# Projections, scores and transposes as pairs of half-row products

## The chip, the core and the metric

The kernel runs on one core of a Trainium2 chip, as one launch. TensorE multiplies, and writes its sums to eight banks of the accumulation memory, of 512 fp32 columns by 128 rows each. VectorE (DVE), ScalarE (ACT) and GpSimd (POOL) do the elementwise work, and all transfers are issued by SyncE (SP). The metric is the time of one execution on the device, in microseconds (us). Of the kernel before there are three runs: 823.28 us in the median, from 822.88 to 824.9.

## What is computed

One layer of a hybrid encoder, for 1024 prompt rows and 32 sample rows of width 1024, all in fp32. Cut to what matters:

```
hn = rmsnorm(h, g_pre)
qA kA vA gA qB kB vB gB = split(hn @ w_in)      # 8 parts of 512 columns
# A: 8 heads of 64, each 64-row chunk sees itself and the 8 chunks before
sA = qA @ kA.T / 8 + bias[clip(k_pos - q_pos, -128, 128)]
oA = softmax(where(in_band, sA, -1e30)) @ vA
# B: 8 heads of 64, strictly causal
z  = qB @ kB.T / 8
w  = sigmoid(z) * product of sigmoid(-z) over the later causal keys
oB = w @ vB
y  = concat(oA * silu(gA), oB * silu(gB)) @ w_out
h  = h + rmsnorm(y, g_post)
h  = h + sigmoid(h @ w_ple_gate) * (p @ w_ple)
```

The k and v of both halves are outputs too. The sample rows also attend to 512 cached keys per head.

## The kernel before

**Precision.** An fp32 matrix enters TensorE as two fp32r parts, an upper part `h` (the value rounded) and a lower part `l` (what rounding left over). A product of two such matrices is the sum of three: upper by upper, upper by lower, lower by upper.

**Projections.** The normed input, transposed, lies in three chunks `hnh[c]`, `hnl[c]` of 352 columns (1056 rows of prompt and sample). A kind (`kA`, `qA`, `vA`, `gA` and so on) and a head pair `p` give 128 output columns. `col_steps` (line 616) makes one kind of one head pair: for each chunk 24 products (3 combinations by 8 blocks of 128 input features) are summed in one bank with the tag `mm`, then ACT copies it to a staging tile `st`. With 32 kind-and-pair combinations and 3 chunks there are 96 such units, 2304 products. For a gate kind, the unit ends in a sigmoid, a multiplication on DVE, one on POOL by the attention's output, and a store.

**Attention.** `prep_k`, `prep_q`, `prep_v` (lines 560 to 582) lay out one head. A head is 64 wide, so q's upper and lower part are stacked in 128 rows (`L`), and k's upper part stands in both halves of `kd`, k's lower part in both halves of `kl`: one product with `kd` and one with `kl` give all combinations. For each block of 128 queries, `scores` (703) multiplies against all its key blocks: up to 5 in A, up to 8 in B, in one piece of up to 512 columns or in two. In A, DVE adds the bias and takes the maximum, ACT exponentiates, POOL scales. In B, DVE adds the mask, ACT takes two sigmoids, DVE runs a scan (the product over later keys), POOL multiplies. `weights_t` (746) transposes the resulting weights on TensorE, block by block of 128x128 against the identity `ident`, and ACT and DVE split the result into `wTh` and `wTl`. `values` (773) sums the weights by v over key blocks in the bank `PV`.

**Transposes elsewhere.** `turn_x` (521) transposes the normed input, `token_major` (587) the k and v that are stored, `sample_attention` (815) the cached k and its weights.

**Banks.** `PS_BUFS` (406) gives two banks to `mm`, three to scores `S`, two to transposes `T`, one to `PV`.

**Order.** All operations are recorded by `Recorder` and then put in order by its `order` (307): a planner that simulates the engines with fixed prices (`cost`, 274) and takes the ready operation of each engine by key. On TensorE attention has the key 0 and projections the key 1, so projections fill what attention leaves. Every recorded operation is issued from line 385, so all rows of the profile carry that line and are told apart by tile names. `weave` (1117) interleaves the attention of head pair n with the projections of pair n+1; pairs 0 to 3 are A, 4 to 7 B. `share = {7: 8}` (1051) places all eight gate combinations in the last pair's stretch, since it has no next pair. The last two gates are recorded after all attention (`GATE_NEEDS`), because their last multiplication needs the attention's output.

**After attention** come the output product and the gated embedding product, blocked into seven smaller products each (`o0P` to `o3P`, `g0P` to `g3P`, tags `ple`, `o`, `g`). The change leaves them as they are, but for the names of two bank tags.

Of the kernel before, what the change touches and what calls it, by code (L numbers as in the profile page):

```python
# [20 lines left out]
KD = 8  # L21
# [13 lines left out]
PARTS = 4  # L35
BEHIND = 2
# [120 lines left out]
class Op:  # L157
    __slots__ = ("eng", "what", "args", "kw", "key", "busy", "late", "ready", "left", "after", "at", "size", "shared")
# [5 lines left out]
ISSUE = 450  # L164
DMA_NS, DMA_RATE, DMA_MARGIN = 1500, 320.0, 800
# [34 lines left out]
class Recorder:  # L200
# [35 lines left out]
    def node(self, eng, what, args, kw, after):  # L236
        o = Op()
        o.eng, o.what, o.args, o.kw, o.after = eng, what, args, kw, after
        o.key = (self.cls if eng == "PE" else self.low, len(self.ops))
        o.shared = False  # L240
        self.ops.append(o)
        return o

    def add(self, eng, what, args, kw):
        writes, reads = [], []
        method = what[1] if isinstance(what, tuple) else ""
        for i, a in enumerate(args):
            if isinstance(a, (View, Raw)):
                (writes if i == 0 or (method == "tensor_tensor_reduce" and i == 7) else reads).append(a)
# [17 lines left out]
        o.busy, o.late = self.cost(eng, method, args, kw, writes, reads)  # L267
        o.shared = eng == "POOL"
# [38 lines left out]
    def order(self):  # L307
# [16 lines left out]
        out, port, line = [], 0.0, 0.0  # L324
        while len(out) < len(self.ops):
# [15 lines left out]
            if o.shared and e == "DVE" and port > t + DVE_SET:  # L341
                held = [x for x in now[e] if not x[2].shared]
                if held:
# [4 lines left out]
                    o = pick[2]  # L348
            o.at = t
# [25 lines left out]
    def emit(self, tc):  # L375
        ops = self.order()
        with tc.manual_schedule():
# [13 lines left out]
def stream_step(  # L391
# [14 lines left out]
    PS_BUFS = {"mm": 2, "S": 3, "T": 2, "PV": 1}  # L406

    def psum(tag, name):
        return ps.tile([P, 512], F32, tag=tag, name=name, bufs=PS_BUFS[tag])
# [31 lines left out]
    )  # L441
    masks = const.tile([P, NS], F32, tag="masks", name="masks")
# [64 lines left out]
    TURN = {}  # L507
# [13 lines left out]
    def turn_x(t, sq, n):  # L521
        for kh in range(2):
            pt = psum(TURN.get((t, kh), "T"), f"ptx{t}_{kh}")
# [31 lines left out]
    KDh, KLD, Lq, V2 = {}, {}, {}, {}  # L555
# [31 lines left out]
    def token_major(ab, p, src, nm, b0, then):  # L587
# [3 lines left out]
        def turn(g0):  # L591
# [3 lines left out]
            pt = psum("T", f"pt{nm}{ab}{p}_{g0}")  # L595
            if g0 < 8:
                for b in range(4):
                    nc.tensor.transpose(pt[:, b * P:(b + 1) * P], src()[:, (g0 + b) * P:(g0 + b + 1) * P], ident)
                nc.scalar.copy(out[:, g0:g0 + 4, :], pt.rearrange("p (b c) -> p b c", b=4))
            else:  # L600
                nc.tensor.transpose(pt[0:NS, 0:P], src()[:, SEQ:T], ident)
                nc.scalar.copy(out[0:NS, 8, :], pt[0:NS, 0:P])
                then(out)

        return [(0.43 if g < 8 else 0.1, lambda g=g: turn(g)) for g in range(b0, 9, 4)]
# [9 lines left out]

    def col_steps(j):

# [3 lines left out]
        box = {}  # L621
        steps = []

        def mms(c, part):
            if part == 0:
                if c == 0:
                    ensure(j)
                    ensure(j + 1)
                    if k != "g":
                        box["st"] = at2.tile([P, T], F32, tag="stg", name=f"st{kind}{p}", bufs=3)  # L630
                box["acc"] = psum("mm", f"mm_{kind}{p}_{c}")[:, 0:CH]
            acc = box["acc"]
            cs = slice(c * CH, (c + 1) * CH)
            if k == "g" and part == 0:
                box["og"] = at2.tile([P, CH], F32, tag="bias", name=f"og{kind}{p}_{c}", bufs=2)
                dma(box["og"], o_dr[n][:, cs])
            W = loaded[j]
            for x in range(part * 24 // PARTS, (part + 1) * 24 // PARTS):
                q, k8 = x // KD, x % KD
                a = W[k8 // 4][1 if q == 1 else 0]  # L640
                b = (hnl if q == 2 else hnh)[c]
                nc.tensor.matmul(acc, a[:, k8 % 4, :], b[:, k8, :], start=(x == 0), stop=(x == 23))
            if part < PARTS - 1:
                return
            if k == "g":
                sg = at2.tile([P, 512], F32, tag="sg", name=f"sg{kind}{p}_{c}", bufs=3)[:, 0:CH]
                nc.scalar.activation(sg, acc, AF.Sigmoid)
                nc.vector.tensor_tensor(sg, acc, sg, ALU.mult)
                nc.gpsimd.tensor_tensor(sg, sg, box["og"], ALU.mult)
                dma(og_dr[n, :, cs], sg)  # L650
            elif k == "q":
                nc.scalar.activation(box["st"][:, cs], acc, AF.Copy, scale=SCALE)
            else:
# [1059 lines left out]
```

## Time and profile before

| | |
|---|---|
| median of three runs | 823.28 us |
| profiled execution | 822.59 us |
| its span (first to last instruction) | 820.8 us |
| TensorE products | 4926, busy 811.7 us |
| TensorE weight loads | 4926, busy 751.1 us |
| DVE, ACT, POOL busy | 601.8, 496.1, 508.3 us |
| granted TensorE clock | 1.0 |
| moved by transfers | 127.19 MB |

Every product on TensorE is a pair of instructions: a weight load (PEld), which puts one matrix of up to 128 rows by 128 columns into the array, and the product itself (PE), which streams the columns of the other through it. A load can run under the product before it. In a row of the timeline `128*128 128x352` means 128 active rows by 128 active columns, and 352 streamed columns; `32*128 32x32` has 32 active rows. The ends of products are modelled, and neighbours overlap in the record, so the distance from start to start is read, and not the length of a single one. In the view of groups the columns are busy time, mean length in ns, then the engine's idle time before.

By the names of the tiles: the projections of the first head pair run to 63.5 us, attention from there to 590.8 us with projections between, the gates until 624 us (from 496.6 us), and the output and gate products to the end.

### The profile page before, as it was taken

Reading aid. Unit: us, or ns where it says so; the run is one execution under the profiler, and the core shown is the slowest. Engines: PE = TensorE matmul, PEld = TensorE weight load, DVE = VectorE, ACT = ScalarE, POOL = GpSimd, SP = SyncE. Lnnn points to the kernel's source line nnn. Section 1 sums busy time; section 2 is a strip of 40 time slices with the busy share of each in tenths; the row PEclk is TensorE's granted clock in tenths of the full one; section 3 lists DMA queues with packets and bytes.
Section 4 is the critical chain, followed back from the end, with each engine's and each line's share of the span. In section 5 each row is a group of like instructions: output and inputs, shape, how many; then the busy total and the mean of one; then the engine's idle time right before and its main releaser. Section 6 shows DMA issues by size and latency. Waiting matters only on the chain.

```text
span 820.8 us, 14862 instructions
## 1 busy us (share of the span) xinstructions
PE 811.7 (99%) x4926; PEld 751.1 (92%) x4926; DVE 601.8 (73%) x1197; ACT 496.1 (60%) x1145; POOL 508.3 (62%) x559
## 2 busy tenths in 40 slices
PE   9999999999999999999999999999999999999997
PEld 7999999999999999999999999999998787888786
DVE  6718886776677688898988889985654676686755
ACT  6624745655636667756665775663437966886741
POOL 6526775585766486675657856676463437599513
PEclk9999999999999999999999999999999999999999
DMA  9327544574545563312333233253479847749733
GB/s 309 109 70 249 145 143 146 146 204 146 147 120 171 144 174 96 85 33 67 105 89 82 50 105 92 83 150 111 135 258 303 287 143 243 251 156 362 245 117 128
DMA packets 113279, 127.19 MB, mean 155 GB/s; under 512 B 10850, under 2 KB 80266, under 8 KB 113203
## 3 DMA queue, kind: packets, MB, share of 16 engines
q1 hardware_dynamic: 113202, 126.24, 50.5%
q8 instruction: 39, 0.64, 0.3%
q14 instruction: 38, 0.30, 0.1%
HBM read 81.21 MB, written 36.59 MB: 144 GB/s over the span
## 4 chain that ended last, share of the span: by engine, by line
PE 94%; DVE 2%; POOL 1%; ACT 1%; DMA 1%; issue 0%; SPq 0%; DVEq 0%
PE mm_kB L385 6%; PE mm_gA L385 6%; PE mm_qA L385 6%; PE mm_kA L385 6%; PE mm_gB L385 5%; PE mm_qB L385 5%; PE mm_vA L385 5%; PE mm_vB L385 5%; PE PVB L385 4%; PE SB L385 4%; PE ptwB L385 4%; PE SA L385 4%; PE PVA L385 4%; PE ptwA L385 3%; PE g1P L385 2%; PE o3P L385 2%
## 5 line engine op out<-in xcount | busy, mean ns | idle before, releaser
L385 POOL TENSOR_TENSOR beB<-beB,omB 128x128 f32<-128x128 f32 (+7 forms) x64 | 87.5, 1373 | 78.6 <-DVE omB L385 25.0
L385 DVE TENSOR_TENSOR_SCAN omB<-omB 128x128 f32<-128x128 f32 (+7 forms) x64 | 100.1, 1575 | 4.4 <-ACT omB L385 2.2
L385 POOL TENSOR_SCALAR beA<-beA,statA 128x640 f32<-128x640 f32 (+2 forms) x64 | 44.3, 696 | 48.6 <-DVE statA L385 47.0
L385 ACT CAST wThA<-ptwA 128x128 fp32r<-128x128 f32 (+3 forms) x96 | 40.1, 424 | 37.4 <-PE ptwA L385 36.5
L385 ACT CAST wThB<-ptwB 128x512 fp32r<-128x512 f32 (+3 forms) x96 | 44.9, 487 | 24.7 <-PE ptwB L385 23.2
L385 ACT ACTIVATE omB<-SB 128x384 f32<-128x384 f32 (+5 forms) x96 | 47.4, 507 | 18.9 <-DVE SB L385 8.1
L385 DVE TENSOR_TENSOR wTlB<-ptwB,wThB 128x512 fp32r<-128x512 f32 (+3 forms) x96 | 50.7, 547 | 9.0 <-ACT wThB L385 7.2
L385 DVE TENSOR_TENSOR wTlA<-ptwA,wThA 128x128 fp32r<-128x128 f32 (+3 forms) x96 | 45.6, 485 | 15.7 <-ACT wThA L385 15.0
L385 ACT ACTIVATE beA<-omA,statA 128x640 f32<-128x640 f32 (+2 forms) x64 | 44.7, 699 | 9.4 <-DVE statA L385 3.5
L385 ACT ACTIVATE beB<-SB 128x384 f32<-128x384 f32 (+5 forms) x96 | 46.6, 506 | 3.4 <-DVE Vl2sB L385 2.0
L385 PE MATMUL ptwB<-ident,beB 128*128 128x128 f32 x288 | 45.0, 273 | 0.1
L385 PE MATMUL ptwA<-ident,beA 128*128 128x128 f32 x240 | 41.5, 273 | 0.0
L385 PEld LDWEIGHTS ptwB<-ident,beB 128*128 128x128 f32 x288 | 35.1, 140 | 2.3 <-issue 0.4
L385 PE MATMUL SB<-kdB,LB 128*128 128x384 f32 (+5 forms) x96 | 34.1, 358 | 0.5 <-ACT beB L385 0.5
L385 DVE CUSTOM_DVE_ANT_0 omA<-SA,biasA 128x320 f32<-128x320 f32 (+2 forms) x64 | 30.8, 481 | 4.5 <-PE SA L385 3.8
L385 PE MATMUL SB<-klB,LB 128*128 128x384 f32 (+5 forms) x96 | 33.4, 349 | 0.0
L385 PEld LDWEIGHTS ptwA<-ident,beA 128*128 128x128 f32 x240 | 30.7, 140 | 1.4 <-issue 0.2
L385 POOL TENSOR_TENSOR oB<-oB,oB 128x256 f32<-128x256 f32 x32 | 25.4, 815 | 10.2 <-issue 5.6
L385 PE MATMUL SA<-kdA,LA 128*128 128x320 f32 (+2 forms) x96 | 31.2, 332 | 0.5 <-DVE LA L385 0.4
L385 POOL TENSOR_TENSOR gB<-gB,gB 128x256 f32<-128x256 f32 x32 | 27.5, 878 | 6.3 <-DMA gB<-in_w_ple_gate_dram 6.1
L385 PE MATMUL SA<-klA,LA 128*128 128x320 f32 (+2 forms) x96 | 30.4, 324 | 0.0
L385 POOL TENSOR_TENSOR h<-h,x 128x512 f32<-128x512 f32 (+1 forms) x18 | 23.4, 1320 | 0.8 <-DVE h L385 0.8
(706 smaller groups left out, 2698.1 us busy)
## 6 DMA issues: line engine op xcount, KB each, us to landing
x<-in_x_prompt_dram SPq DMA_DIRECT2D x8, 512.0 KB, 5.5
oB<-in_w_out_dram SPq DMA_DIRECT2D x16, 256.0 KB, 4.5
sum_dro<-oB SPq DMA_DIRECT2D x16, 256.0 KB, 2.2
gB<-in_w_ple_gate_dram SPq DMA_DIRECT2D x16, 256.0 KB, 4.3
sum_drg<-gB SPq DMA_DIRECT2D x16, 256.0 KB, 2.1
x<-in_x_prompt_dram SPq DMA_DIRECT2D x16, 256.0 KB, 3.8
h_dr<-h SPq DMA_DIRECT2D x8, 512.0 KB, 3.5
ht<-h_dr SPq DMA_DIRECT2D x8, 512.0 KB, 5.1
```

Source lines behind the costliest of these rows:

```text
L385: getattr(getattr(tc.nc, o.what[0]), o.what[1])(*args, **kw)
```

## The change

**Half rows.** TensorE's array can be used as two halves of 64 rows, and the change issues most products as pairs: one product on rows 0 to 63, one on rows 64 to 127, each with a bank of its own (`pair`). Three kinds of work become pairs.

- A projection unit's 24 products are cut into 48 half products. Low rows and high rows of one pair belong to different units (`triple`): three units are open at once, and the high rows run `BEHIND` = 12 slots behind. A unit has one bank. It is summed first by one half of the rows, 24 products, and then by the other, and between them stands a `relay`: a one-element memset on POOL that waits for the last product of the one, and for which the first product of the other waits. There are three `mm` banks.
- A block of scores is three pairs (upper-upper, upper-lower, lower-upper): the low rows hold q against the first 64 keys of each key block, the high rows against the other 64. `prep_k` reorders k for this with two transfers, `prep_q` copies q's parts into the other half of the rows with two. The scores lie in two banks side by side (`SS`), and with more than four key blocks they take both whole.
- A transpose of a 128x128 block is two of 64 rows (`turn`), whose results lie in two banks (`TT`), in halves of 256 columns used in turn.

ACT's and DVE's instructions on scores and transposes span both banks, and where a block of scores had two pieces there is one instruction now. A bias of the A heads is loaded in two parts, in 64-column runs.

**Order.** The planner adds `CHANGE` = 170 when TensorE goes between half rows and full rows; the products of one `values`, and of one block of scores, are kept together (`together`, `in_turn`). The planner's prices for pairs are 158 for a projection, 61 for a transpose, and at least 107 for scores.

**Gates.** One gate each goes to the stretches of pairs 4, 5 and 6, and five stay in the last. The k and v transposes of a kind come two steps into the next kind's projections.

The transposes of the first three input tiles, of the sample rows' input and of the last phase, all values and the output products stay in full rows. The diff, cut to its core:

```diff
-PARTS = 4
-BEHIND = 2
+STEPS = 12
+BEHIND = 12
...
+    def pair(self, first, second, busy):
+
+        both = [x for x in (first, second) if x]
+
+        def emit(*real):
+            for i, (method, _, _, _, more) in enumerate(both):
+                more = dict(more)
+                bank = more.pop("bank", None)
+                done = getattr(self.tc.nc.tensor, method)(*real[3 * i:3 * i + 3], **more)
+                if bank is not None:
+                    if bank.count == 24:
+                        self.wait(done, bank.relay, "the other half of the rows has written this bank")
+                    bank.count, bank.last = bank.count + 1, done
+
+        args = [v for x in both for v in x[1:4]]
+        self.add("PE", emit, args, {})
+        self.ops[-1].busy = busy
+        return self.ops[-1]
...
+    def relay(self, bank, buf):
+
+
+        def emit(real):
+            bank.relay = self.tc.nc.gpsimd.memset(real, 0.0)
+            self.wait(bank.relay, bank.last, "a bank is handed to the other half of the rows")
...
+            if e == "PE" and o.mode != mode:
+                t, mode = t + CHANGE, o.mode
...
-    PS_BUFS = {"mm": 2, "S": 3, "T": 2, "PV": 1}
+    PS_BUFS = {"mm": 3, "PV": 1}
+    TT, SS = (TwoBanks(rec, ps, x) for x in ("TT", "SS"))
+    LOW, HIGH = slice(0, HD), slice(HD, P)
+    second = []
...
+    def turn(out, src, x):
+
+        n = src.shape[1]
+        rec.pair(*(("transpose", out[0:n, a, x * HD:(x + 1) * HD], src[r], ident[r, r], {}) for a, r in enumerate((LOW, HIGH))), 61)
...
     def prep_k(nm, h, st):
-        r, o = halves(h)
-        kd = opnd[h].tile([P, SEQ], F32R, tag=f"kd{h}", name=f"kd{nm}{h}")
-        kl = opnd[h].tile([P, SEQ], F32R, tag=f"kl{h}", name=f"kl{nm}{h}")
-        nc.vector.tensor_copy(kd[r], st[r, 0:SEQ])
-        nc.gpsimd.tensor_tensor(kl[r], st[r, 0:SEQ], f(kd[r]), ALU.subtract)
-        dma(f(kd[o]), f(kd[r]))
-        dma(f(kl[o]), f(kl[r]))
-        KDh[h], KLD[h] = kd, kl
+
+        K = opnd[h].tile([P, 2, 512], F32R, tag=f"L{h}", name=f"K{nm}{h}")
+        raw = wpool.tile([P, 512], F32, tag="wr", name=f"rk{nm}{h}", bufs=4)
+        src = st[h * HD:(h + 1) * HD, 0:SEQ].rearrange("p (b a k) -> p b a k", b=8, a=2)
+        for a, r in enumerate((LOW, HIGH)):
+            dma(raw[r].rearrange("p (b k) -> p b k", b=8), src[:, :, a, :])
+        nc.vector.tensor_copy(K[:, 0], raw)
+        nc.gpsimd.tensor_tensor(K[:, 1], raw, f(K[:, 0]), ALU.subtract)
+        Kq[h] = K
 
     def prep_q(nm, h, st):
         r, o = halves(h)
-        L = opnd[h].tile([P, SEQ], F32R, tag=f"L{h}", name=f"L{nm}{h}")
-        nc.vector.tensor_copy(L[r], st[r, 0:SEQ])
-        nc.vector.tensor_tensor(L[o], st[r, 0:SEQ], f(L[r]), ALU.subtract)
-        Lq[h] = L
+        qh = opnd[h].tile([P, SEQ], F32R, tag=f"kd{h}", name=f"qh{nm}{h}")
+        ql = opnd[h].tile([P, SEQ], F32R, tag=f"kl{h}", name=f"ql{nm}{h}")
+        nc.vector.tensor_copy(qh[r], st[r, 0:SEQ])
+        nc.vector.tensor_tensor(ql[r], st[r, 0:SEQ], f(qh[r]), ALU.subtract)
+        dma(f(qh[o]), f(qh[r]))
+        dma(f(ql[o]), f(ql[r]))
+        Lq[h] = (qh, ql)
...
+    def products(items):
+
+        for low, high in items:
+            behind.append(high)
+            x = [low, behind.pop(0)]
+            turned = [y[0].relay for y in x if y and y[0].count == 24]
+            now = rec.pair(*(y and y[0].product(y[1], r) for y, r in zip(x, (LOW, HIGH))), 158)
+            now.after.update(turned)
+            for y in x:
+                if y and y[0].count == 24:
+                    y[0].relay = rec.relay(y[0].bank, said)
+                if y and y[0].count == 48:
+                    y[0].end()
+
+    def triple(units):
+
+        low = [(u, x) for u in units for x in range(24)]
+        high = [(u, x) for u in (units[2], units[0], units[1]) for x in range(24)]
+        todo = list(zip(low, high))
+        m = len(todo) // STEPS
+        return [todo[m * t:m * t + m] for t in range(STEPS)]
...
+    def in_turn(begin):
+
+        rec.together(begin)
+        mine = [o for o in rec.ops[begin:] if o.eng == "PE"]
+        mine[0].after.update(scored)
+        scored[:] = mine[-1:]
...
-                bias = at2.tile([P, 640], F32, tag="bias", name=f"bias{nm}", bufs=2)
-                dma(bias, bias_src(2 * p + h, P, 0, 640))
-                nc.gpsimd.memset(bias[0:HD, 0:HD], NEG)
-                nc.gpsimd.memset(bias[HD:P, 576:640], NEG)
+                bias = at2.tile([P, 2, 320], F32, tag="bias", name=f"bias{nm}", bufs=2)
+                src = bias_src(2 * p + h, P, 0, 640).ap
+                for a in range(2):
+                    part = bass.AP(tensor=src.tensor, offset=src.offset + a * HD, ap=[[1, P], [P, 5], [1, HD]])
+                    dma(bias[:, a, :].rearrange("p (x k) -> p x k", k=HD), Raw(r_dr, part))
+                nc.gpsimd.memset(bias[0:HD, 0, 0:HD], NEG)
+                nc.gpsimd.memset(bias[HD:P, 1, 256:320], NEG)
                 box["bias"] = bias
 
...
-            L, kd, kl = Lq[h], KDh[h], KLD[h]
+            q, K = Lq[h], Kq[h]
             b0 = lo_block(i)
-            n = (i + 1 - b0) * P
-            k0 = b0 * P
-            cut = [0, n] if n <= 512 else [0, n // 2, n]
+            m = i + 1 - b0
+            n = m * P
             w0 = at.tile([P, SEQ + 1], F32, tag="om", name=f"om{nm}_{i}", bufs=3)
             w1 = at.tile([P, SEQ], F32, tag="be", name=f"be{nm}_{i}", bufs=3)
-            pieces = []
-            for j in range(len(cut) - 1):
-                s = psum("S", f"S{nm}_{i}_{j}")[:, 0:cut[j + 1] - cut[j]]
-                lhs = L[:, i * P:(i + 1) * P]
-                ks = slice(k0 + cut[j], k0 + cut[j + 1])
-                nc.tensor.matmul(s, lhs, kd[:, ks], start=True, stop=False)
-                nc.tensor.matmul(s, lhs, kl[:, ks], start=False, stop=True)
-                pieces.append((cut[j], cut[j + 1], s))
+            s = (SS.half if m <= 4 else SS.both)(f"S{nm}_{i}")[:, :, 0:m * HD]
+            lhs, ks = slice(i * P, (i + 1) * P), slice(b0 * HD, (i + 1) * HD)
+            begin = len(rec.ops)
+            for x, (y, z) in enumerate(((0, 0), (0, 1), (1, 0))):
+                more = dict(start=x == 0, stop=x == 2)
+                rec.pair(*(("matmul", s[:, a, :], q[y][r, lhs], K[r, z, ks], more) for a, r in enumerate((LOW, HIGH))), max(107, 5 + 0.4167 * m * HD))
+            in_turn(begin)
...
                 nc.gpsimd.memset(w0[:, n:n + 1], 1.0)
-                for a, b, s in pieces:
-                    nc.scalar.activation(w0[:, a:b], s, AF.Sigmoid, scale=-1.0)
-                for a, b, s in pieces:
-                    nc.scalar.activation(w1[:, a:b], s, AF.Sigmoid)
+                nc.scalar.activation(rows(w0[:, 0:n]), sv, AF.Sigmoid, scale=-1.0)
...
-                pt = psum("T", f"ptw{nm}_{i}_{j}")
+                pt = TT.half(f"ptw{nm}_{i}_{j}")
                 for x in range(m):
-                    nc.tensor.transpose(pt[:, x * P:(x + 1) * P], w1[:, (b - b0 + x) * P:(b - b0 + x + 1) * P], ident)
-                hi, lo = wT[g, j]
...
-    share = {7: 8}
+    share = {4: 1, 5: 1, 6: 1, 7: 5}
```

More of the change, by code (lines that the diff above doesn't have):

```diff
@@ new lines, in triple, with flush @@
+    def triple(units):
[4 more added lines that the diff above has]
+        return [todo[m * t:m * t + m] for t in range(STEPS)]
+    def flush():
+        rest = [(None, None)] * BEHIND
+        return [(0.95, lambda: products(rest[0:6])), (0.95, lambda: products(rest[6:]))] + [x for t in tails[0:1] for x in t]
+    def col_steps(j):
+        kind, p = order[j]
+        need = GATE_NEEDS.get((kind, p))
+        steps = [(0.95, lambda x=x: products(x), need if i == 0 else None) for i, x in enumerate(triple([Unit(j, c) for c in range(NCH)]))]
+        if tails:
+            steps[2:2] = tails.pop(0)
+        if kind[0] != "g":
+            tails.append(tail(j))
+        return steps
@@ L620, in col_steps @@
         n = sidx(ab, p)
[L621 to L653, printed above, removed]
-                nc.scalar.copy(box["st"][:, cs], acc)
@@ L1234, in stream_step @@
     ensure(2)
-    first = [col_steps(j) for j in range(3)]
+    first = [triple([Unit(j, c) for j in range(3)]) for c in range(NCH)]
     for c in range(NCH):
@@ L1239, in stream_step @@
                 norm_tile(t, *(xs.get(t) or load_x(t)), GPRE)
-        for j in range(3):
-            for st in first[j][PARTS * c:PARTS * (c + 1)]:
-                st[1]()
+        for x in first[c]:
+            products(x)
     for x in ple.later:
```

262 lines of the change are left out of this document (195 added, 67 removed).

## The prediction

> **What bounds the kernel now.** I read the page's busy times and slices first, then the chain that ended last, then TensorE's list of waits, and last the pieces of the chain and the timeline, where the pace of one kind of product can be read.
>
> ```profile
> PE 811.7 (99%) x4926; PEld 751.1 (92%) x4926; DVE 601.8 (73%) x1197; ACT 496.1 (60%) x1145; POOL 508.3 (62%) x559
> PEclk9999999999999999999999999999999999999999
> PE 94%; DVE 2%; POOL 1%; ACT 1%; DMA 1%; issue 0%; SPq 0%; DVEq 0%
> PE idle L385 <- DVE newh L385: 1.3, 1, 1.3
> PE PVsB L385 <- DVE Vl2sB L385: 0.9, 2, 0.5
> ```
>
> TensorE is busy 811.7 of 820.8 us at the full granted clock, makes 94% of the chain, and the two largest sums in its list of waits are 1.3 and 0.9 us. So the span is TensorE's instructions laid end to end, and a change is priced by what it takes from or adds to that row of instructions. A mean duration of a product overlaps its neighbours; the pace is what counts, and merged runs give it:
>
> ```profile
> 32.33 3.90 PE mm_vA L385 x24
> 703.63 0.87 PE pth L385 x8
> 779.88 2.80 PE g3P L385 x12
> ```
>
> A 352-column projection product takes 3.90/24 = 0.1625 us, a 512-column one 2.80/12 = 0.233 us, a transpose of a 128x128 fp32 block 0.87/8 = 0.109 us. Between the first two a column costs 0.00044 us, so 320, 384 and 448 columns cost 0.148, 0.176 and 0.205 (worked out). Short products have a floor, the weight load:
>
> ```profile
> 302.33 0.19 PEld L385 LDWEIGHTS PVA<-wThA,v2A 128*128 128x128 f32 x1
> 302.44 0.30 PEld L385 LDWEIGHTS PVA<-wTlA,v2A 128*128 128x128 f32 x2
> 5.61 0.29 PEld L385 LDWEIGHTS gpre<-ghl,ones 1*128 1x128 f32 x2 [0.17 <-issue]
> 743.16 0.57 PEld L385 LDWEIGHTS pth<-ident,ht 32*128 32x128 f32 x8 [0.37 <-PE g1P L385]
> L385 PEld LDWEIGHTS ptwB<-ident,beB 128*128 128x128 f32 x288 | 35.1, 140 | 2.3 <-issue 0.4
> ```
>
> Two loads for fp32r products start 0.30 - 0.19 = 0.11 us apart with 128 rows, and 0.29 - 0.19 = 0.10 us apart with one row: the load's time does not shrink with the rows. Loads for transposes of 32 rows start (0.57 - 0.14)/7 = 0.061 us apart.
>
> **The change part by part.** In the order in which the changed program stands, TensorE has 8362 products instead of 4926: 4608 half-row projection products (2304 before), 816 half-row score products (384), 1456 half-row transposes in place of 728 full ones. Values, output and gate products stay full.
>
> *Projections.* 2304 full products become 2304 pairs of 352 columns, plus 12 slots because the second halves run 12 behind. If the two halves of a pair run side by side, a pair costs what one costs now, 0.1625. Bounds: below, 0.155 (a half streams the same 352 columns, so no gain beyond a few ns of issue); above, two loads one after the other, 2 x 0.11 = 0.22. I take 0.1625, because the 352 columns cover one load (0.11) with 0.05 to spare and the halves use different rows and banks: +12 x 0.1625 = +1.9 us. No row of this trace shows two halves at once; this is the large unknown.
>
> The TensorE page of the Trainium skill ("TensorE: Matmul & The Clock Gate", LDWEIGHTS) says that load time depends on the columns and not on the rows; the one-row load above agrees, and this speaks against the change, since a pair has two loads of full length. The skill's "TensorEngine Tiling (Array Packing)", Key Properties, says that different tiles load and multiply in parallel. By the second the term is +1.9, by the first with the loads in a row it is the rival below, +132.
>
> *Scores.* Before, q's upper and lower parts were stacked in 128 rows against k's upper part and then its lower part: 2 products over all n columns. Now three pairs (upper-upper, upper-lower, lower-upper) over n/2 columns in each half. Per A head before: 2 x (0.11 + 0.120 + 0.176 + 0.233) for the first four blocks, and 4 blocks of two pieces of 320, 16 x 0.148, together 3.65 us; after: 3 x (0.11 + 0.11 + 0.11 + 0.12 + 4 x 0.148) = 3.13. Per B head before 4.33, after 3 x (0.33 + 0.12 + 0.148 + 0.176 + 0.205 + 0.233) = 3.64. Eight heads each: -4.2 - 5.5 = -9.7 us.
>
> *Transposes.* A half takes 64 rows and streams 64 columns. I take 0.061 a pair, the pace of the 32-row transposes, which also stream fewer columns; the upper end is 0.122 (two such loads in a row), the lower 0.055 (half of 0.109). 728 x (0.109 - 0.061) = -34.9 us, from +9.5 to -39.
>
> *Going between half rows and full rows.* The program order has 116 changes between the two kinds (58 visits), most at the value products. Before had few of them, and one can be measured:
>
> ```profile
> 742.83 0.40 PE L385 MATMUL g1P<-gT,wlS2g 128*128 128x512 f32 x1
> 743.16 0.68 PE L385 MATMUL pth<-ident,ht 32*128 32x32 f32 x8
> 743.77 0.73 PE L385 MATMUL g0P<-gT,S3g 128*128 128x512 f32 x2
> ```
>
> The last full product holds TensorE 0.33 us where 0.233 is its pace (+0.10). The eighth 32-row transpose starts near 743.16 + 0.68 - 0.22 = 743.62 (0.22 is such a transpose's length) and the next full product 0.15 later, not 0.065 (+0.09). That product's successor comes 0.73 - 0.40 = 0.33 later (+0.10: a load was not hidden). So 0.29 a visit, and 0.06 more for the visit's own first load: 0.35 x 58 = +20.3 us. Bounds: 0.19 (drains alone) gives 11, 0.41 (two exposed fp32r loads of 0.11) gives 24.
>
> *The handing over of a bank.* Each of the 96 projection units sums 24 half products from one half of the rows and then 24 from the other. Between them the change puts a one-element memset on POOL that waits for TensorE, and the other half's first product waits for it.
>
> ```profile
> L385 POOL TENSOR_TENSOR beB<-beB,omB 128x128 f32<-128x128 f32 (+7 forms) x64 | 87.5, 1373 | 78.6 <-DVE omB L385 25.0
> L385 POOL MEMSET omB<- 128x1 f32 x16 | 1.4, 97 | 0.4
> L385 POOL TENSOR_TENSOR klB<-stkB,kdB 64x1024 fp32r<-64x1024 f32 x2 | 6.8, 3376 | 1.0 <-PE ptwB L385 1.0
> ```
>
> The lag of 12 pairs is 12 x 0.1625 = 1.95 us. A memset (0.10) behind one average POOL operation (1.37) still comes in time; behind one of 3.38 it is 1.5 late. While the memset waits, POOL's multiplications queue behind it, and the weight transposes wait for those. Bounds 0 and 96 x 1.4 = 134; near the lower one because the lag exceeds the average operation: +4 us (0.04 each).
>
> *On other engines, counted as nothing.* Score activations and reductions over two banks become one instruction where they were two, the prepared k works on 128 rows x 512 (64 x 1024 before), which shortens DVE, ACT and POOL. Against that, k now comes through two SBUF transfers before its split, q's copies in the other half through two after it, and a bias through two with 256-byte runs: SP has 18 more rows. The cover is the next pair's projections, about 35 us a head pair (216 x 0.1625); without it each of 16 preparations would show a transfer, 2.2 us by the page's landing time of a 256 KB one:
>
> ```profile
> sum_dro<-oB SPq DMA_DIRECT2D x16, 256.0 KB, 2.2
> 432.60:496.60 64.00, 63.91 (x418) 61.35 (x417) 55.51 (x83) 43.06 (x105) 43.06 (x44) 1.00 0.28 73
> 496.60:591.00 94.40, 94.03 (x610) 91.09 (x609) 73.48 (x110) 51.09 (x119) 63.14 (x63) 1.00 0.40 116
> ```
>
> *Gates between heads.* The sum of gate products stays; what matters is who is late next. The two windows (columns: span, then busy PE, PEld, DVE, ACT, POOL) are a B head pair with projections and the last one with gates. DVE needs 55.5 of 64 us. A B pair loses 72 x 0.048 + 1.4 = 4.9 us of TensorE work, which would bring DVE near the bound, but gets a gate, 72 x 0.1625 = 11.7. The last pair loses three gates, 35.1 + 4.9 of its 94.4, and DVE's 73.5 would exceed the 54 left; the products of the last two gates (23.4) need nothing of attention and can fill it. So 0; were they not able to, 73.5 - 54.4 - 5 of DVE's gate work = +14.
>
> Sum, on the profiled execution's 822.6 us (span 820.8, 1.8 around it): 822.6 + 1.9 - 9.7 - 34.9 + 20.3 + 4 = 804.2. That execution is 0.7 us below the median 823.28, so 804 to 805 as a median: faster by 2.3%.
>
> **The rivals.**
> 1. *The halves' loads do not run side by side* (the other side). Then a projection pair costs 0.22, a transpose pair 0.122, every score pair below 512 columns 0.22. 2304 x 0.0575 = +132; transposes +9.5 instead of -34.9; scores 384 x 0.22 + 24 x 0.233 - 63.8 = +26; with 1.9 + 20.3 + 4: 1016 us. It decides as soon as a projection pair takes 804's gain, 18.4 us over 2316 pairs, 8 ns more than 0.1625. For it: one-row loads take full length. Against it: a pair's halves share neither rows nor bank.
> 2. *The transposes gain nothing*: four instructions in the time of two. If a pair needs 0.109 as the block does now, 804 + 35 = 839. For it: nothing in this trace goes faster for long than the 0.061 of the 32-row loads, a load and a product each. Against it: the first product after a block of transposes starts 0.03 us behind it, so single starts are not the limit.
> 3. *The handing over waits.* 0.19 us at each of 96 eats the gain; at 0.5 us it is 848. For it: POOL is 62% busy with operations up to 3.4 us. Against: 1.95 us of lag.
> 4. *The last head pair runs on DVE*: 804 + 14 = 818, still faster.
>
> **How the numbers follow.** Sum as worked out, with rival 4 and the bounds of the visits, 0.70 (own range 790 to 820); rival 1 0.12; rival 2 0.08; rival 3 0.07, of which 0.03 still ends faster; no change within 0.3%, which a measurement here could hardly tell from none, 0.03. Faster 0.73, same 0.03, slower 0.24. The range 788 to 845 takes in rivals 2 and most of 3 and leaves out rival 1 and a few per cent below.
>
> **What would show it.** Right: low and high half products start within some ns of each other and 24 pairs of mm take 3.9 us; four pairs of a transpose take about 0.25 us; TensorE still near 99% busy with few waits; about 0.35 us more around each block of value products. Wrong: pairs of mm 0.2 us apart, mm products that wait for POOL's memset, score products that wait for ACT or DVE because five and more blocks now hold both score banks (two before, of three), or idle TensorE in the last head pair.

## The result, and the profile after

The changed kernel takes 876.82 us (875.43 to 878.08, 4 runs) against 823.89 us (822.88 to 824.9, 4 runs) for the kernel before on the same chip: a ratio of 1.064 [1.062, 1.066]. It is slower by 6.4%; 804 had been forecast. The profiled execution's span is 875.0 us, 54.2 longer than the 820.8 of before.

The page of the changed kernel (busy time and share of each engine; busy tenths of TensorE in 40 slices and its granted clock; the chain that ended last, by engine):

```profile
span 875.0 us, 21850 instructions
PE 827.5 (95%) x8362; PEld 729.2 (83%) x8362; DVE 581.3 (66%) x1133; ACT 495.9 (57%) x1081; POOL 491.0 (56%) x655
PE   8899899888999999999999999999999999899997
PEclk9999899999999999999999999999999999999999
PE 54%; DVE 6%; ACT 5%; POOL 4%; issue 3%; DMA 3%; SPq 0%; POOLq 0%; DVEq 0%; ACTq 0%
```

TensorE was busy 99% and is busy 95%; it made 94% of the chain and makes 54%, and ScalarE and VectorE stand in the chain with 11%. Of the 820.8 us before TensorE was not busy for 9.1, of the 875.0 after for 47.5: 38.4 of the 54.2 us are TensorE standing. The granted clock, 0.993 over the whole span, accounts for 6 us at most (0.007 x 875). TensorE's list of waits (who waits, for what; us in all, times, longest) says where the chain leaves TensorE:

```profile
PE TT L302 <- DVE wTlA L484: 5.3, 10, 0.9
PE TT L302 <- ACT wThA L484: 4.9, 11, 0.8
PE TT L302 <- DVE wTlB L484: 4.0, 8, 0.9
PE TT L302 <- ACT wThB L484: 3.1, 8, 0.7
PE SS L302 <- DMA qlA<-qlA: 3.0, 1, 3.0
PE TT L484 <- ACT lg L484: 1.8, 3, 0.7
```

Before, the largest sum was 1.3 us. The first four are transposes (into TT) that wait for ScalarE's and VectorE's instructions of *another* group of transposes (wTh and wTl are what those two write while they read TT). A transpose's own input is not among them. In every one of these 37 waits the reader is at the other half of the same two banks, never at the half that is about to be written (worked out from the trace and the built program).

That the halves run side by side is in the timeline of the same kernel (start, duration, engine, line, product; low and high half of a pair below each other):

```profile
300.14 0.32 PE L302 MATMUL mm_qB<-hnl,wh_qB 64*128 64x352 f32 x1
300.14 0.32 PE L302 MATMUL mm_qB<-hnh,wl_qB 64*128 64x352 f32 x1
300.30 0.32 PE L302 MATMUL mm_qB<-hnl,wh_qB 64*128 64x352 f32 x1
300.31 0.32 PE L302 MATMUL mm_qB<-hnh,wl_qB 64*128 64x352 f32 x1
...
300.79 0.22 PE L302 MATMUL TT<-ident,stkB 64*32 64x64 f32 x2
300.81 0.41 PE L302 MATMUL mm_qB<-hnh,wh_qB 64*128 64x352 f32 x1
300.82 0.41 PE L302 MATMUL mm_qB<-hnh,wl_qB 64*128 64x352 f32 x1
301.06 0.32 PE L302 MATMUL mm_qB<-hnh,wh_qB 64*128 64x352 f32 x1
```

A pair of projections starts every 0.16 us, here with both halves within 0.01 us. But behind a pair of transposes the second projection pair starts 0.25 us after the first (300.81 to 301.06).

A group of three blocks shows the new wait. In this stretch of the changed kernel's timeline the rows of the transposes and their readers are kept:

```profile
233.28 0.34 PE L302 MATMUL TT<-ident,beA 64*128 64x64 f32 x4 [0.49 <-DVE statA L484]
...
233.65 0.38 ACT L484 CAST wThA<-TT 128x256 fp32r<-128x256 f32 x1 [0.23 <-PE TT L302]
...
234.30 0.34 PE L302 MATMUL TT<-ident,beA 64*128 64x64 f32 x5
...
234.87 0.42 DVE L484 TENSOR_TENSOR wTlA<-TT,wThA 128x256 fp32r<-128x256 f32 x1
...
235.32 0.48 ACT L484 CAST wThA<-TT 128x384 fp32r<-128x384 f32 x1 [1.30 <-DVE wTlA L484]
...
235.56 0.32 PE L302 MATMUL mm_qA<-hnh,wh_qA 64*128 64x352 f32 x1
...
235.84 0.56 DVE L484 TENSOR_TENSOR wTlA<-TT,wThA 128x384 fp32r<-128x384 f32 x1 [0.48 <-ACT wThA L484]
...
236.54 0.28 PE L302 MATMUL TT<-ident,beA 64*128 64x64 f32 x2 [0.66 <-DVE wTlA L484]
```

Nothing that touches TT overlaps: products, ScalarE's copy and VectorE's subtraction go one at a time, in the order of the program, whichever half they use. The group at 234.30 stands ahead of the first group's subtraction (234.87) in the program, so it is written first, and the subtraction and the next copy follow one by one. The next transposes (236.54) come only behind VectorE's read (235.84 + 0.56 = 236.40), and TensorE, which works in order, starts nothing between 235.56 and 236.54, six projection pairs' worth. In the kernel before, TensorE writes the next group (219.03 to 219.63) while VectorE still reads the one before it (219.20 to 219.75), because the next group lies in the other bank:

```profile
218.25 0.47 ACT L385 CAST wThA<-ptwA 128x384 fp32r<-128x384 f32 x1
...
219.03 0.60 PE L385 MATMUL ptwA<-ident,beA 128*128 128x128 f32 x4
...
219.20 0.55 DVE L385 TENSOR_TENSOR wTlA<-ptwA,wThA 128x384 fp32r<-128x384 f32 x1
```

Where the time went, from the start of each run of products of one kind to the start of the next run of another kind, summed over each trace (worked out from all TensorE instructions, us, up to the start of the last run; a wait counts to the kind that stands ahead of it; the third column is an experiment below):

| kind | before | after | before, one tile |
|---|---|---|---|
| projections | 390.0 | 425.9 | 402.6 |
| transposes | 76.9 | 78.7 | 119.5 |
| scores | 74.8 | 73.1 | 78.6 |
| values | 71.6 | 81.5 | 76.2 |
| all else | 199.8 | 208.1 | 204.6 |

After minus before is 35.9 + 1.8 - 1.7 + 9.9 + 8.3 = 54.2, the whole difference of the spans. Transposes and scores, which were to give 44.6 us, give nothing between them (+1.8 and -1.7), and the projections, in which those visits lie, are 35.9 longer.

### The profile page after: what moved, and what is told of

Its sections match the earlier page's. It is cut to its first block, busy times and chain, and to the rows that moved or that the text cites. A ratio compares the mean times of both kernels' runs of the same rounds, so it can differ in the third digit from the quotient of the medians.

```text
span 875.0 us, 21850 instructions
## 1 busy us (share of the span) xinstructions
PE 827.5 (95%) x8362; PEld 729.2 (83%) x8362; DVE 581.3 (66%) x1133; ACT 495.9 (57%) x1081; POOL 491.0 (56%) x655
## 4 chain that ended last, share of the span: by engine, by line
PE 54%; DVE 6%; ACT 5%; POOL 4%; issue 3%; DMA 3%; SPq 0%; POOLq 0%; DVEq 0%; ACTq 0%
PE TT L302 5%; PE mm_vB L302 5%; PE SS L302 4%; PE mm_kB L302 4%; PE mm_gA L302 4%; PE PVB L484 4%; PE mm_qB L302 4%; PE mm_gB L302 3%; PE PVA L484 2%; PE g2P L484 2%; PE g3P L484 2%; PE g0P L484 2%; PE mm_vA L302 2%; PE g1P L484 2%; POOL h L484 2%
## 5 line engine op out<-in xcount | busy, mean ns | idle before, releaser
L484 DVE TENSOR_TENSOR wTlA<-TT,wThA 128x128 fp32r<-128x128 f32 (+3 forms) x96 | 45.6, 488 | 37.0 <-ACT wThA L484 20.9
L484 DVE TENSOR_TENSOR wTlB<-TT,wThB 128x512 fp32r<-128x512 f32 (+3 forms) x96 | 51.3, 550 | 23.0 <-ACT wThB L484 12.6
L484 ACT CAST wThB<-TT 128x512 fp32r<-128x512 f32 (+3 forms) x96 | 45.2, 485 | 36.1 <-PE TT L302 25.9
L321 POOL MEMSET said<- 1x1 f32 x96 | 9.8, 102 | 96.2 <-PE mm_vA L302 19.4
L484 ACT ACTIVATE omB<-SS 128x128 f32<-128x128 f32 (+7 forms) x64 | 41.8, 654 | 37.8 <-DVE SS L484 31.9
L484 ACT ACTIVATE beB<-SS 128x128 f32<-128x128 f32 (+7 forms) x64 | 41.9, 655 | 3.6 <-PE TT L302 1.6
L302 PE MATMUL mm_qA<-hnh,wl_qA 64*128 64x352 f32 x192 | 41.3, 340 | 0.0
L302 PE MATMUL mm_qA<-hnl,wh_qA 64*128 64x352 f32 x192 | 41.2, 337 | 0.0
L302 PE MATMUL mm_qB<-hnh,wh_qB 64*128 64x352 f32 x192 | 41.1, 333 | 0.0
L302 PE MATMUL mm_gA<-hnl,wh_gA 64*128 64x352 f32 x192 | 40.7, 330 | 0.0
L302 PE MATMUL mm_qB<-hnl,wh_qB 64*128 64x352 f32 x192 | 40.3, 330 | 0.0
```

The costliest lines, as they stand in the source:

```text
L302: done = getattr(self.tc.nc.tensor, method)(*real[3 * i:3 * i + 3], **more)
L321: bank.relay = self.tc.nc.gpsimd.memset(real, 0.0)
L484: getattr(getattr(tc.nc, o.what[0]), o.what[1])(*args, **kw)
```

## The experiments

The theory from this reading: **a group of transposes now takes both banks of TT, so the two banks that were used in turn are one buffer, and an order planned for two makes TensorE stand.** In the program as built, 343 waits of transposes on other engines stand before products into TT: 117 are for the input, 26 for a reader of the same half, and 200 for a reader of the other half or the other bank (some 20 of these for the other bank). The rivals: the gates' new place; GpSimd, which stands 96.2 us at the hand-over memsets; the changes between half and full rows and the uncovered weight loads alone.

**1. The old kernel with its two transposes banks as one tile.**

```
+    TT = TwoBanks(rec, ps, "TT")
...
+        if tag == "T":
+            return TT.bank(name)
         return ps.tile([P, 512], F32, tag=tag, name=name, bufs=PS_BUFS[tag])
```

`TwoBanks` declares one tile of [P, 2, 512], and `bank` gives its two banks in turn.

> The kernel before, with its two banks for transposes declared as one tile of two banks, as in the changed kernel: the same whole products and transposes in almost the same order on every engine, but a group of transposes now waits until ScalarE and VectorE have read the group before it, because every use of one tile is put in order. Theory (the changed kernel lost the second buffer of the transposes, and its order counts on one): the loss shows here without any pair, 850 to 885 us, with waits of transposes on the readers (wTh, wTl) of 25 us or more in the list of waits. Rival (the pairs themselves, the changes between half and full rows and the weight loads that nothing covers): nothing of this is in here, 822 to 830 us.

Measured: 890.94 us (890.85 to 891.04), ratio to before 1.083 [1.080, 1.086], so 68 us slower, a little beyond the theory's range, without one half-row product. Its page and list of waits:

```profile
PE 840.0 (94%) x4926; PEld 751.0 (84%) x4926; DVE 597.0 (67%) x1197; ACT 503.2 (57%) x1145; POOL 499.0 (56%) x559
PE TT L427 <- ACT wThB L427: 7.9, 15, 0.7
PE TT L427 <- DVE wTlA L427: 5.6, 12, 0.8
PE TT L427 <- ACT wThA L427: 4.3, 13, 0.5
PE TT L427 <- DVE wTlB L427: 3.1, 6, 0.8
```

It has the signature of the changed kernel: TensorE from 99% to 94%, and the same four waits, 20.9 us here (25 or more had been expected) and 17.3 there. There is one difference: all 46 of them here are for a reader of the other bank, where in the changed kernel the reader is at the other half of the same banks. Either way TensorE can no longer write one group while another is being read. The order of TensorE's products is that of before up to the 2178th and nearly so behind. So the second buffer of the transposes is worth 68 us to an order that counts on it; this takes in the last phase, which is 5.3 us longer here. Against this kernel the changed one, in which the two banks are one tile too, is 14 us faster. That is the pairs and all else in the change together; the gates' new place alone is worth some 7 in experiment 7.

**2. Half the hold.** VectorE's subtractions out of TT are left out:

```
-                nc.vector.tensor_tensor(lo, src, f(hi), ALU.subtract)
+                rec.add("DVE", lambda *real: None, (lo, src, f(hi)), {})
...
```

The order keeps a place for the subtraction, but nothing is issued there. A second edit, not shown, lets the products with the values take the upper part twice.

> The changed kernel without VectorE's 192 subtractions for the lower part of the attention weights: the products with the values take the upper part twice (so the lower part is left out of the result). TensorE's products are as many as before and in the same order; the banks of the transposes are held for one reader instead of two, about 1.0 instead of 1.75 us, and VectorE has 97 us less to do. Theory (banks held): the waits of transposes on wTh and wTl fall from 17 us to under 6, and the time to 840 to 860 us. Rival (the changes, the uncovered loads, the gates): 868 to 880 us.

Measured: 859.16 us (857.85 to 860.47), ratio 1.044 [1.040, 1.048]: 18 us less than the changed kernel. The waits of transposes on wTl are gone; those on wTh are 7.5 us, where under 6 had been expected:

```profile
PE TT L302 <- ACT wThA L484: 4.4, 11, 0.7
PE TT L302 <- ACT wThB L484: 3.1, 9, 0.5
```

From the first product of a group to the end of its last read a group of the attention's weights takes 1.59 us in the mean, 2.90 in the changed kernel (worked out from the traces). It speaks for the theory, though not for it alone: VectorE also has 192 instructions less.

**3. The same, with the subtraction kept but fed from SBUF.**

```
-                nc.vector.tensor_tensor(lo, src, f(hi), ALU.subtract)
+                rec.add("DVE", lambda out, _, part: tc.nc.vector.tensor_tensor(out, part, part, ALU.subtract), (lo, src, f(hi)), {})
```

> The changed kernel with every instruction in the same place, but VectorE works out the lower part of the attention weights from the upper part alone (upper minus upper) and no longer reads the bank of the transposes. So the lower parts of the attention weights are left out of the result; the number of instructions is the same on every engine. Theory (the bank of the transposes is held until ScalarE and then VectorE have read it, and the next group of transposes waits for that although it writes the other half): a hold ends one VectorE instruction and one semaphore earlier, some 0.7 us of about 1.75, so most of the waiting at transposes goes: 835 to 855 us instead of 877, and the waits of products into TT on VectorE's wTl tiles (9.3 us after) go to under 2. Rival (the gates between heads cost it), rival (POOL stands waiting at the hand-over memsets and brings weights late) and rival (only the changes between half and full rows and the uncovered weight loads cost it): nothing of theirs is touched, 873 to 881 us.

Measured: 886.38 us (885.19 to 887.57), ratio 1.076 [1.072, 1.081]: 10 us *slower* than the changed kernel. The expectation failed. A group is through as soon as in experiment 2 (1.56 us), and the waits of transposes on wTl are gone here too, but the groups of costly instructions (count, busy us, mean ns) show that the edit made VectorE slow; first the changed kernel, then this one:

```profile
L484 DVE TENSOR_TENSOR wTlB<-TT,wThB 128x512 fp32r<-128x512 f32 (+3 forms) x96 | 51.3, 550 | 23.0 <-ACT wThB L484 12.6
```

```profile
L956 DVE TENSOR_TENSOR wTlB<-wThB 128x512 fp32r<-128x512 f32 (+3 forms) x96 | 86.7, 915 | 12.2 <-ACT wThB L484 10.7
```

With both operands in SBUF the subtractions of the B heads take 915 instead of 550 ns in the mean of their four shapes, and VectorE has 56 us more to do (637.6 busy instead of 581.3). TensorE's waits at transposes for a reader of another group fall to 7 us, but its waits at scores rise from 5 to 13 us and those at transposes for anything else from 13 to 22 (worked out from the lists of waits). As a test of the theory it is inconclusive.

**4. The last phase.** Every second bank of transposes there comes from another tile:

```
+        if second and tag == "T":
+            second.append(True)
+            tag = "PV" if len(second) % 2 else tag
```

> The changed kernel with every second transposes bank of the last phase taken from the bank of the values (another tile) instead of from the pair. Theory (even the two whole banks of the pair are ordered as one tile): the last phase goes from 204.9 back to about 198 us and the time to 867 to 872 us. Rival (the last phase is longer for its weights or its reads of the memory, which come late): 875 to 880 us.

Measured: 870.42 us (868.09 to 872.74), ratio 1.058 [1.051, 1.065]: 6.4 us less than the changed kernel. Behind the last projection product 201.2 us are left, 204.9 in the changed kernel and 196.9 before, so 3.7 of the 8 us that the last phase had lost are back (some 198 us had been expected), and the waits on lg are gone. There the transposes are whole ones into single banks, so for these 3.7 us it is only that the two banks are one tile that made them wait.

**5. Fewer and larger groups.**

```
+            pt = (TT.half if n <= 4 else TT.both)(f"ptw{nm}_{i}")
+            for x in range(n):
+                turn(pt, w1[:, x * P:(x + 1) * P], x)
```

> The changed kernel with all blocks of a unit (up to 8) transposed in one group over both banks in full, where two groups of up to 4 took half of both banks each; the copies to SBUF stay as they were. A head then has 8 groups instead of 12: 64 holds of the banks and 64 visits of transposes among the projections fewer. Theory (banks held, and the load after a visit uncovered): each visit saved is worth some 0.2 us of waiting and 0.18 us of edges, so 845 to 862 us. Rival (only the gates or the hand-over memsets cost it): 870 to 880 us.

Measured: 879.61 us (878.24 to 880.98), ratio 1.069 [1.065, 1.073]: no gain, and the theory's number is missed by 17 us. The projections are 9.5 us shorter (416.4 us in the table's measure), but transposes, scores and all else are 12 longer. The part that the theory names did shrink: the waits at transposes for a reader of another group fall from 17.6 to 9.0 us, and the time in which some group of the attention's weights lies in TT from 405 to 353 us. What grew in its place are TensorE's waits at scores (from 5 to 10 us) and those at transposes for anything else (from 13 to 19 us; all worked out from the traces). Why these grew was not tried. So the theory's price per group was wrong: a wait that is taken away at one place can come back at another.

**6. An order that knows.** A half of TT or SS is taken by the order to hold the whole pair, first with the spare time that the order keeps ahead of a product (400 ns), then without it:

```
-        cells = [... for c in (0, 1) if c0 < 256 * c + 256 and c1 > 256 * c]
+        cells = [... for c in (0, 1)]
```

> The changed kernel with one line of the order's bookkeeping changed: a half of the pair of banks is taken to hold the whole pair until it is read, as the built program does. The instructions are the same, only their order moves. Theory (the order was written for halves that can be used in turn, and TensorE, which works in order, stands where they can't): with an order that knows it, the waiting at transposes falls from some 45 us in the list of waits to under 25, and the time to 835 to 865 us; the number of changes between half and full rows may rise, each visit costing 0.35 us. Rivals (gates, hand-over memsets, changes and loads alone): 870 to 885 us, as much waiting elsewhere.

```
-MARGIN = 400
+MARGIN = 0
```

> The changed kernel, its order made as in the one that knows that a half of the pair of banks is the whole (1008 us), and without the 400 ns that the order keeps free ahead of every product that waits for another engine. If the loss lay only in an order that did not know of the holds, an order that knows them and keeps no time free comes to 830 to 855 us. Theory (the chain product, ScalarE, VectorE, next product of one pair of banks is by itself about as long as the work of a head, so that no order hides it): 870 to 930 us.

Measured: 1008.24 us (ratio 1.224 [1.220, 1.228]) and 966.45 us (1.173 [1.168, 1.178]). Both are worse than the order that does not know. So telling this planner of the hold does not mend the loss, and the theory's numbers, 835 to 865 and 870 to 930, are both too low. The reason for the second miss is in its page (TensorE's busy tenths and granted clock):

```profile
PE   8999997889998889999679899985799689999997
PEclk9999997699999699999679999995899879999999
```

In the 20th slice TensorE starts 10 projection products and in the 28th none, where the slices ahead of them have 230 and 136 (counted in the trace): the projections of that stretch have run out while the attention, whose groups go through the banks one at a time, is still under way. TensorE is busy 6 and 5 tenths of these two slices, and the clock granted in them is 6 and 5 tenths; its mean over the span is 0.921 (0.903 with the spare time kept). I had counted the waiting and not the clock. That the chain of holds bounds the attention by itself, so that an order that keeps to it only moves the waiting to where nothing else is left to do, would fit this, but no run shows it, and for the transposes' banks one trace speaks against it: in the kernel of 1008 us no two groups in TT overlap, and all groups together fill 471 of the 681 us between the attention's first and last, so the pair is free in the rest.

**7. The gates.** All gates back at the last head in the changed kernel, and the new shares alone in the kernel before:

```
-    share = {4: 1, 5: 1, 6: 1, 7: 5}
+    share = {7: 8}
```

> The changed kernel with all gates back at the last head, as before. Theory (banks of the transposes held): the first head pair and the pairs of the first half of the heads lose their 8 and 20 us in any case, since no gate lies there; 868 to 888 us. Rival (the gates' new place costs the time): 825 to 845 us, the changed kernel less most of its 53 us.

> The kernel before with the gates between the heads alone, and every product and transpose whole as it was. Theory (banks held): the gates are worth little by themselves, 818 to 830 us. Rival (the gates' new place costs the time): 845 to 877 us.

Measured: 883.74 us (ratio 1.073 [1.069, 1.077]), and 823.62 us against 824.03 (0.999 [0.998, 1.001]). The rival falls on both sides: the new place is worth nothing in the old kernel and some 7 us of *gain* in the new one. That a gate there gives TensorE something to do between two groups would explain it; this was not tried apart.

**8. The hand-over on another engine.**

```
-            bank.relay = self.tc.nc.gpsimd.memset(real, 0.0)
+            bank.relay = self.tc.nc.scalar.copy(real, real)
```

> The changed kernel with the 96 hand-overs of a bank between the halves of the rows on ScalarE (a copy of one element) instead of GpSimd (a memset of one element). GpSimd no longer stands 96 us in all at the memsets. Rival (GpSimd stands at the hand-overs and brings the weights and the attention's scaling late): 845 to 865 us. Theory (banks of the transposes held; GpSimd is not waited for): 872 to 885 us, a little longer rather, since ScalarE, which reads those banks, is the one that stands then.

Measured: 887.24 us (885.34 to 889.13), ratio 1.077 [1.072, 1.083]: 10 us slower, a little beyond the theory's range and far from the rival's. In the changed kernel the memset and those who waited for it are:

```profile
L321 POOL MEMSET said<- 1x1 f32 x96 | 9.8, 102 | 96.2 <-PE mm_vA L302 19.4
```

```profile
who waited for it (us, times):
  ACT omB L484: 1.9, 1
  PEld TT L302: 1.0, 1
  PEld mm_kA L302: 0.3, 1
```

GpSimd stands 96 us at the hand-overs, but most of that time is spare: 3.2 us in all are waited for directly behind them, 0.3 of it by a projection. On ScalarE, a reader of the transposes' banks, the hand-overs cost 10 us more.

## Why the prediction was wrong

- **Projections, right in the pace.** A pair costs 0.160 us (0.1625 taken), the halves side by side. Rival 1 (1016 us) is refuted, and so is the reason that rival 2 gave: four pairs of transposes take 0.22 us from the first to the next projection. What rival 2 says of the outcome, that the transposes gain nothing, came true for another reason (below).
- **Going between half and full rows, right.** The 108 changes seen in the trace cost 21.9 us beyond the products' pace, some waits among them; 20.3 had been taken. Part of the 9.9 us of the values' row lies here.
- **The hand-over of a bank, right in kind.** The term was 4 us, and 3.2 are waited for behind the memsets; rival 3 is refuted.
- **Gates and other engines, right as nothing** in the old kernel (experiment 7), with one exception in the new one: of k's and q's new transfers, counted as covered, one is waited for 3.0 us in the first head pair.
- **Transposes: the step that failed.** The sum has 728 x (0.109 - 0.061) = -34.9 us, a pace alone. It reads what a block costs while transposes follow each other and leaves out what a visit costs at its ends, and above all that each group takes both banks. With that the prediction's first premise went too, that the span is TensorE's instructions laid end to end: TensorE stands 47.5 us instead of 9.1. The next table has the visits with transposes of the attention's weights that follow a projection and are followed by two or more. It gives the time from the start of the last projection ahead to that of the second behind, less two paces of 0.160, per trace:

| kernel | visits | blocks | us | ns per block |
|---|---|---|---|---|
| before | 77 | 241 | 27.3 | 113 |
| after | 100 | 300 | 45.1 | 150 |
| before, one tile | 80 | 246 | 48.5 | 197 |
| after, upper part only | 98 | 290 | 34.9 | 120 |

 A pair of transposes in use costs 150 ns, more than the whole transpose that it replaces (113). Without any wait the median visit of four blocks in the changed kernel is 0.163 + 0.216 + 0.250 - 0.320 = 0.309 us, 77 ns a block: 61 for the pace and 16 for the way out of the visit, where the second projection starts 0.250 us behind the first. (Before the change it starts 0.246 behind the first too, but the first one follows so soon on the four long transposes, 0.355 us after the start of the first of them where their pace makes 0.436, that the visit costs 0.441 in all.) So of the 89 ns above the forecast's 61, about a fifth is the way out, and the rest is waiting.
- **Scores, mis-sized too.** -9.7 us were forecast and -1.7 came. From its start to that of the next product a pair of 64 to 256 columns takes 129 to 166 ns in the mean, where 110 to 120 had been taken. TensorE also waits 5 us ahead of scores in the changed kernel, 3.0 of them for the transfer just named, and 1 before. The prediction had named score products that wait because blocks of five and more hold both score banks, as a sign of error, and gave it no price; the same thought about the transposes, whose every group holds both banks, is missing. How much of the loss is the score banks' own hold and how much that of the transposes was not tried apart.
- **The last phase** was counted as untouched. It lost 8 us, and experiment 4 gives 3.7 of it back; the rest stays open.

Put together: experiment 1 prices the lost buffer at 68 us in the old kernel, and 876.8 - 804.2 = 72.6 us is what the prediction missed. The two numbers come from different kernels, and that they lie so close is in part luck. What is shown is that the loss of the second buffer alone costs the old kernel 68 us, and that the changed kernel waits at the same places for the same readers. That it is the larger part of the miss there is inferred from this: apart from the last phase (experiment 4), no run gives the changed kernel its second buffer back.

Two sections of the Trainium skill bear on it. "TensorEngine Tiling (Array Packing)", Gotcha 1: PSUM Pressure, says that different row tiles write to different banks; that is why a group of four half-filled pairs takes two banks where it took one, and the table above has the price, 150 ns a block instead of 113. "PSUM — Partial Sum Buffer", in the section on bank collisions, says that TensorE's write and another engine's read must be kept apart by bank (and quadrant of 32 partitions) and not by address; by it, TensorE could not have written one half of a bank while ScalarE or VectorE read the other half in the same partitions. The trace agrees in so far as the 37 waits above are all for a reader at the other half of the same bank, and no two uses of TT overlap in the stretch above (233.28 to 236.40); no run here lets them.

## What to carry to other kernels

Before costing work in halves of the array, count the banks that one group of results holds and for how long: pairs fill two banks where whole products fill one, and in these programs a bank is free again only when its last reader is through. Look also at what the program declares: in experiment 1, and in the last phase of the changed kernel, each group needed only one bank, and the next one waited because the two banks were one tile. If the same number of banks served as two buffers before, the price of losing one (here 68 us of 823) stands against the whole gain in pace. And take the price of short products from whole visits, from the last long product ahead to the second one behind, since the pace leaves out the way out of the visit and every wait at its start.

## What the runs showed that I had not expected

- The granted clock was lowest where TensorE stood most: 0.921 and 0.903 in the two kernels of experiment 6, with single slices granted 5 to 7 tenths, but 0.993 in the changed kernel, whose waits for wTh and wTl are 0.9 us at most.
- VectorE's 128x512 subtraction of two SBUF operands (B heads, experiment 3) took 1014 ns in the mean, against 683 with one of them in PSUM. The fastest took the same time in both, 654 and 653 ns, but half of them took over 836 ns, and the longest 2377 against 693. Why was not tried.
- The second product behind transposes starts about 0.25 us after the first whether the transposes are whole (109 ns each) or in pairs (61 ns): this cost belongs to the way out of a visit, not to the transposes' length.
